# Two buffers for an expert tile's weighted output rows, and half the scratch for dynamic DMAs

## The chip, the cores and the metric

The kernel runs on one core of a Trainium2 chip. The metric is the device time of one execution in microseconds. Before the change it is 2016.36 us, the median of three runs (2011.74 to 2021.05).

## The reference

A backbone of two layers over 256 latent tokens and 256 context tokens of 1024 channels, one batch. Each layer has a token mixer (a state space, a gated MLP over chunks, differential attention, merged by gates) and then a mixture of experts. The change touches the experts alone, and of the reference they are this, for `h` of 512 tokens in the first layer and the 256 latent ones in the second:

```python
scores = jax.nn.sigmoid((h @ w_router).astype(jnp.float32))
...
_, eidx = lax.top_k(jnp.where(emask, sel, -jnp.inf), TOP_K)
wts = jnp.take_along_axis(scores, eidx, axis=1)
wts = wts / jnp.sum(wts, -1, keepdims=True) * ROUTED_SCALE
routed = routed_experts(h, eidx, wts.astype(h.dtype), w_exp_gate, w_exp_up, w_exp_down)
return routed + swiglu(h, w_sh_gate, w_sh_up, w_sh_down)
```

There are 64 experts of hidden width 256, and each token goes to 8 of them. An expert's result for a token is `(silu(x @ wg) * (x @ wu)) @ wd`, times the token's weight, and a token's results are added up. All of it is float32.

## The kernel before, in words

**Tiles.** After the router, `route` sorts the (token, expert) pairs by expert into units of 32 rows and packs four units into a tile of 128 rows. The four units use three lanes (`LANE_OF = (0, 0, 1, 2)`), so a tile takes rows of at most three experts. Large experts and small ones alternate in the order: the largest, the smallest, the second largest, and so on. With the given inputs the first layer (layer 0) has 38 tiles, the second (layer 1) 20. Per tile there is a column of token numbers to gather (`tb["gather"]`) and one of rows to add to (`tb["scatter"]`).

**Weights.** An expert's three matrices, 3 MB, are loaded by SP into one of four slots of a ring `raw` (L1226; the three DMAs of one load stand together). `load_next` (L1598) waits until the slot's former expert has been copied out (`s_cp`, L1601), and the loop at L1604 holds SP until all loads but the last have landed, so at most two are in flight.

**One tile, `body` (L1654).** On TensorE: the gate and up matmuls of tile t (`gate_up`, L1630), the transposes of tile t+1's rows (`x_t`, L1622), the transposes of the hidden values (`h_t`, L1639), then the down matmuls of tile t-1 (`down`, L1646). TensorE reads weights from `GU` (three buffers of a quarter each, per lane) and `DN` (two buffers), into which DVE (lanes 0 and 2) and ACT (lane 1) copy them from `raw` (L1578, L1584). Which slot a copy reads is loaded into registers first (`sources`, L1558; the register loads show as L1208).

The order on each engine is that of the code. On ACT, per tile: the SiLU activation of t (L1634), two copies for x_t (L1623), the copy of the hidden values (L1640), lane 1's first copy for t+1, then in `down(t-1)` the first half of y (L1648), lane 1's second copy, the second half of y, lane 1's third copy; and in the next `body` lane 1's fourth copy. On POOL, per tile: the gather of the rows of tile t+2 (L1554), then the scatter of tile t-1 (L1651), which adds the 128 rows of `Y` into `acc` in HBM; each lane adds into rows of its own. Both are dynamic DMAs, whose descriptors POOL writes; the scratch for descriptors lies at the start of every partition of SBUF.

`Y` (L1539) is one tile of 4 KB per partition:

```python
Y = pool.tile([P, D], F32, name="y")
...
nc.scalar.activation(Y[:, 512 * hf:512 * hf + 512], pY[hf], AF.Copy, scale=W[t % 4])
```

The framework puts in the waits: the first half of y waits for the landing of the scatter that read `Y` last, the scatter waits for both halves, and since every scatter adds into `acc`, for the one before.

**After the tiles,** `combine` (L1711) reads `acc` back, adds the lanes and normalizes; it begins when the last scatter has landed. In the first layer the next layer's mixer follows.

Of the kernel before, what the change touches and what calls it, by code (L numbers as in the profile page):

```python
# [11 lines left out]
F32 = mybir.dt.float32  # L12
F32R = mybir.dt.float32r
I32 = mybir.dt.int32
AF = mybir.ActivationFunctionType
ALU = mybir.AluOpType
# [5 lines left out]
P = 128  # L22
D = 1024
# [18 lines left out]
LANES = 3  # L42
# [59 lines left out]
class Build:  # L102
# [1418 lines left out]
    def experts(self, l, n, tb, fD, acc, raw):  # L1521
        nc, tc, A = self.nc, self.tc, self.A
# [8 lines left out]
        with tc.tile_pool(name="ex", bufs=1, reuse_waits="tile") as pool, \  # L1531
# [4 lines left out]
            DN = [[pool.tile([P, 2, D], F32, name="dn%d_%d" % (a, b)) for b in range(2)] for a in range(LANES)]  # L1536
            SG = pool.tile([P, EH], F32, name="sg")
            HT = [pool.tile([P, 2, P], F32, name="ht%d" % i) for i in range(2)]
            Y = pool.tile([P, D], F32, name="y")  # L1539
            W = [pool.tile([P, 1], F32, name="w%d" % i) for i in range(4)]  # L1540
            pX = [pp.tile([P, 512], F32, name="px%d" % i) for i in range(2)]
            pG = [pp.tile([P, 512], F32, name="pg%d" % i) for i in range(2)]
# [1 line left out]
            pY = [pp.tile([P, 512], F32, name="py%d" % i) for i in range(2)]  # L1544
# [97 lines left out]
            def down(t, between=()):  # L1642
                for hf in range(2):
                    for k in range(2):
                        for ln, r in rows:
                            nc.tensor.matmul(pY[hf][r, :], HT[t % 2][:, k, r], DN[ln][t % 2][:, k, 512 * hf:512 * hf + 512],  # L1646
                                             start=(k == 0), stop=(k == 1), tile_position=(0, r.start))
                    nc.scalar.activation(Y[:, 512 * hf:512 * hf + 512], pY[hf], AF.Copy, scale=W[t % 4])  # L1648
                    for f in between[hf:hf + 1]:
                        f()  # L1650
                nc.gpsimd.indirect_dma_start(out=acc, out_offset=bass.IndirectOffsetOnAxis(ap=tb["scatter"][:, t:t + 1], axis=0),  # L1651
                                             in_=Y, in_offset=None, bounds_check=LANES * n - 1, oob_is_err=False, compute_op=ALU.add)

            def body(t, sv, sa):  # L1654
                gate_up(t, range(6))
                copies_last(t, sv, sa)
                gate_up(t, range(6, KC))
                act(t)
                more = t + 1 < tmax
                if more:  # L1660
                    x_t(t + 1)
                    sv = sources(t + 1, ET.DVE, range(LANES))
                    for b in range(3):
                        for ln in (0, 2):
                            copy_gu(t + 1, ln, b, sv)
                h_t(t)
                if t + AHEAD < tmax:
                    gather(t + AHEAD)
                between = ()
                if more:  # L1670
                    sa = sources(t + 1, ET.Activation, (1,))
                    copy_gu(t + 1, 1, 0, sa)
                    between = [lambda b=b: copy_gu(t + 1, 1, b, sa) for b in (1, 2)]
                if t > 0:
                    down(t - 1, between)
                else:
                    for f in between:
                        f()
                if more:
                    for ln in (0, 1):  # L1680
                        copy_dn(t + 1, ln, sv)
                return sv, sa

            def rest(t, sv, sa):

                if t < tmax:
                    with tc.If(ntv > t) as more:
                        rest(t + 1, *body(t, sv, sa))
                    with more.Else():
                        down(t - 1)  # L1690
                else:
                    down(t - 1)
# [115 lines left out]
```

## Time and profile before

| | |
|---|---|
| median of the runs | 2016.36 us |
| the profiled execution's own time | 2016.54 us |
| its span in the trace | 2014.5 us |
| TensorE matmuls (PE) busy | 1724.2 us, 86% |
| VectorE (DVE) busy | 1153.1 us, 57% |
| ScalarE (ACT) busy | 792.6 us, 39% |
| GpSimd (POOL) busy | 585.0 us, 29% |
| HBM read and written | 403.16 MB and 55.03 MB |

Times in the trace are microseconds from the span's start. The expert tiles of the first layer run from about 640 to 1215 us, those of the second from about 1660 to 1986; the rest is the mixers, the routing and the combining. In a row of the timeline the first number is the start, the second how long it took, and the bracket at the end says how long the engine was idle before it and what ended that. PEld is TensorE's weight load. A `q` behind an engine's name is its sequencer, which waits and loads registers while the engine itself is idle. A DMA issued by POOL is busy on POOL while its descriptors are written; its landing is another, later time.

### The profile page before, as it was taken

Reading aid. Unit: us, or ns where it says so; the run is one execution under the profiler, and the core shown is the slowest. Engines: PE = TensorE matmul, PEld = TensorE weight load, DVE = VectorE, ACT = ScalarE, POOL = GpSimd, SP = SyncE. Lnnn points to the kernel's source line nnn. Section 1 sums busy time; section 2 is a strip of 40 time slices with the busy share of each in tenths; the row PEclk is TensorE's granted clock in tenths of the full one; section 3 lists DMA queues with packets and bytes.
Section 4 is the critical chain, followed back from the end, with each engine's and each line's share of the span. In section 5 each row is a group of like instructions: output and inputs, shape, how many; then the busy total and the mean of one; then the engine's idle time right before and its main releaser. Section 6 shows DMA issues by size and latency. Waiting matters only on the chain. (4 is left out here: it accounts for less than half of the span.)

```text
span 2014.5 us, 33549 instructions
## 1 busy us (share of the span) xinstructions
PE 1724.2 (86%) x12397; PEld 1009.1 (50%) x12397; DVE 1153.1 (57%) x2295; ACT 792.6 (39%) x1317; POOL 585.0 (29%) x385
## 2 busy tenths in 40 slices
PE   5898999999997988999889763889989689897883
PEld 2686866778865323333323221777779653232231
DVE  7688554333654756766565546663554456655554
ACT  3344343323313544555444343432454224443441
POOL 5355310222201324343233224323042202331222
PEclk8898999999998989999999885889999789998996
DMA  8113524553767555677798937635564567999974
GB/s 273 48 48 116 170 95 139 182 191 134 265 240 309 171 187 182 220 220 242 263 354 313 360 90 269 215 130 183 187 194 130 206 245 275 323 343 354 386 263 122
DMA packets 158391, 435.02 MB, mean 216 GB/s; under 512 B 25813, under 2 KB 82547, under 8 KB 133114
## 3 DMA queue, kind: packets, MB, share of 16 engines
q1 hardware_dynamic: 124716, 344.04, 46.5%
q0 software_dynamic: 17280, 51.93, 10.7%
q10 hardware_dynamic: 16206, 36.66, 5.0%
q8 instruction: 103, 1.69, 0.3%
q14 instruction: 86, 0.70, 0.1%
HBM read 403.16 MB, written 55.03 MB: 227 GB/s over the span
## 5 line engine op out<-in xcount | busy, mean ns | idle before, releaser
L1630 PE MATMUL pg<-gu,xt 128*32 128x512 f32 x3712 | 487.4, 641 | 105.0 <-ACT gu L1578 65.8
L1578 DVE COPY gu<-raw 128x1024 f32 x476 | 298.8, 689 | 160.0 <-issue 82.1
L1651 POOL DMA_INDIRECT acc<-y,t_scatter x58 | 208.8, 3600 | 584.0 <-ACT y L1648 313.1
L1630 PEld LDWEIGHTS pg<-gu,xt 128*32 128x32 f32 x3712 | 141.1, 117 | 438.9 <-issue 238.8
L1578 ACT COPY gu<-raw 128x1024 f32 x238 | 244.3, 1043 | 63.2 <-PE pg L1630 35.7
L1646 PE MATMUL py<-dn,ht 128*32 128x512 f32 x1856 | 211.1, 595 | 2.5 <-ACT gu L1578 1.7
L1584 DVE COPY dn<-raw 128x2048 f32 x178 | 212.9, 1224 | 0.4 <-issue 0.4
L136 PE MATMUL mm<-uh,whi 128*128 128x512 f32 (+1 forms) x544 | 199.3, 366 | 7.9 <-ACT rx L849 4.5
L138 PE MATMUL mm<-uh,wlo 128*128 128x512 f32 (+1 forms) x544 | 194.8, 358 | 0.5 <-DVE wlo L315 0.5
L137 PE MATMUL mm<-ul,whi 128*128 128x512 f32 (+1 forms) x544 | 194.2, 357 | 0.0
L315 DVE TENSOR_TENSOR wlo<-raw,whi 128x1024 fp32r<-128x1024 f32 x77 | 97.0, 1261 | 110.6 <-ACT whi L312 110.2
L312 ACT CAST whi<-raw 128x1024 fp32r<-128x1024 f32 x92 | 96.1, 1047 | 145.3 <-PE mm L137 121.3
L1648 ACT ACTIVATE y<-py,w 128x512 f32<-128x512 f32 x116 | 79.7, 689 | 157.0 <-DMA acc<-y,t_scatter 147.5
L1635 DVE TENSOR_TENSOR sg<-sg,pg 128x256 f32<-128x256 f32 x58 | 24.4, 421 | 195.7 <-ACT sg L1634 195.7
L136 PEld LDWEIGHTS mm<-uh,whi 128*128 128x128 f32 x544 | 106.3, 195 | 33.5 <-issue 8.0
L1634 ACT ACTIVATE sg<-pg 128x256 f32<-128x256 f32 x58 | 22.3, 384 | 250.1 <-PE pg L1630 250.1
L137 PEld LDWEIGHTS mm<-ul,whi 128*128 128x128 f32 x544 | 106.3, 195 | 17.1 <-issue 4.6
L1554 POOL DMA_INDIRECT xg<-f,t_gather x62 | 67.3, 1085 | 162.8 <-DVE t_scatter L1518 68.2
L138 PEld LDWEIGHTS mm<-uh,wlo 128*128 128x128 f32 x544 | 106.1, 195 | 16.1 <-issue 2.3
L1646 PEld LDWEIGHTS py<-dn,ht 128*32 128x32 f32 x1856 | 54.6, 109 | 114.9 <-issue 107.9
L1622 PEld LDWEIGHTS px<-ct,xg 128*128 128x128 f32 x480 | 58.8, 194 | 60.1 <-issue 60.1
L1622 PE MATMUL px<-ct,xg 128*128 128x128 f32 x480 | 70.4, 290 | 9.9 <-DMA xg<-f,t_gather 9.9
(482 smaller groups left out, 2823.1 us busy)
## 6 DMA issues: line engine op xcount, KB each, us to landing
raw<-in_w_exp_gate_dram SPq DMA_DIRECT2D x68, 1024.0 KB
raw<-in_w_exp_up_dram SPq DMA_DIRECT2D x68, 1024.0 KB
raw<-in_w_exp_down_dram SPq DMA_DIRECT2D x68, 1024.0 KB
raw<-in_w_in_dram SPq DMA_DIRECT2D x42, 1024.0 KB
mraw<-in_w_mod_dram SPq DMA_DIRECT2D x80, 512.0 KB
cb_y<-acc SPq DMA_DIRECT2D x18, 512.0 KB
fraw<-in_w_mod_dram SPq DMA_DIRECT2D x16, 512.0 KB
acc<-zt ACTq DMA_DIRECT2D x12, 512.0 KB
```

The costliest lines, as they stand in the source:

```text
L136: nc.tensor.matmul(out, lh, rh, start=start, stop=False)
L137: nc.tensor.matmul(out, lh, rl, start=False, stop=False)
L138: self.last = nc.tensor.matmul(out, ll, rh, start=False, stop=stop).ins
L312: self.nc.scalar.copy(hv, src)
L315: i = eng.tensor_tensor(lv, src, hv.bitcast(F32), op=ALU.subtract)
L1578: c = nc.scalar.copy(dst, gu) if ln == 1 else V.tensor_copy(dst, gu)
L1584: c = V.tensor_copy(DN[ln][t % 2].rearrange("p a b -> p (a b)"), srcs[ln][:, 4096:6144])
L1622: nc.tensor.transpose(pX[hf][:, k * P:(k + 1) * P], XG[t % AHEAD][:, 4 * hf + k:D:8], ident)
L1630: nc.tensor.matmul(pG[t % 2][r, :], XT[:, k, r], GU[ln][(4 * t + k // 2) % 3][:, k % 2].rearrange("p g n -> p (g n)"), start=(k == 0), sto ...
L1646: nc.tensor.matmul(pY[hf][r, :], HT[t % 2][:, k, r], DN[ln][t % 2][:, k, 512 * hf:512 * hf + 512], start=(k == 0), stop=(k == 1), tile_pos ...
L1648: nc.scalar.activation(Y[:, 512 * hf:512 * hf + 512], pY[hf], AF.Copy, scale=W[t % 4])
L1651: nc.gpsimd.indirect_dma_start(out=acc, out_offset=bass.IndirectOffsetOnAxis(ap=tb["scatter"][:, t:t + 1], axis=0), in_=Y, in_offset=None, ...
```

## The change

`Y` becomes two tiles that alternate from one expert tile to the next: `down` writes half by half into `Y[t % 2]`, and the scatter reads that one. The second tile takes 4 KB of every partition. The scratch for descriptors of dynamic DMAs is given as 8192 bytes per partition; without the argument it is 16384.

```diff
-            Y = pool.tile([P, D], F32, name="y")
+            Y = [pool.tile([P, D], F32, name="y%d" % i) for i in range(2)]
...
-                    nc.scalar.activation(Y[:, 512 * hf:512 * hf + 512], pY[hf], AF.Copy, scale=W[t % 4])
+                    nc.scalar.activation(Y[t % 2][:, 512 * hf:512 * hf + 512], pY[hf], AF.Copy, scale=W[t % 4])
...
                 nc.gpsimd.indirect_dma_start(out=acc, out_offset=bass.IndirectOffsetOnAxis(ap=tb["scatter"][:, t:t + 1], axis=0),
-                                             in_=Y, in_offset=None, bounds_check=LANES * n - 1, oob_is_err=False, compute_op=ALU.add)
+                                             in_=Y[t % 2], in_offset=None, bounds_check=LANES * n - 1, oob_is_err=False, compute_op=ALU.add)
...
-    nc = _bacc.Bacc("TRN2", target_bir_lowering=False, num_devices=1)
+    nc = _bacc.Bacc("TRN2", target_bir_lowering=False, num_devices=1, dynamic_dma_scratch_size=8192)
```

## Rows read from the trace of the kernel before

**Rows 1.** The page: the line that writes y, and POOL's DMA queue

```profile
L1648 ACT ACTIVATE y<-py,w 128x512 f32<-128x512 f32 x116 | 79.7, 689 | 157.0 <-DMA acc<-y,t_scatter 147.5
...
q0 software_dynamic: 17280, 51.93, 10.7%
```

**Rows 2.** Busy time by stretch; the last three columns: PE clock, DMA share, GB/s

```profile
650.00:1091.00 441.00, 399.93 (x3254) 142.61 (x3254) 277.88 (x434) 214.14 (x308) 154.00 (x61) 0.96 0.70 234
...
1667.00:1809.00 142.00, 126.95 (x1029) 46.27 (x1029) 89.46 (x140) 68.08 (x99) 44.23 (x18) 0.95 0.86 316
```

**Rows 3.** Waits of L1648 from 650.0 to 1091.2: until what, us, times

```profile
  DMA acc<-y,t_scatter: 71.2, 17
```

**Rows 4.** The timeline of ACT, 787 to 808, in part

```profile
787.67 0.38 ACT L1634 ACTIVATE sg<-pg 128x256 f32<-128x256 f32 x1 [3.74 <-PE pg L1630]
...
798.58 0.69 ACT L1648 ACTIVATE y<-py,w 128x512 f32<-128x512 f32 x1 [7.77 <-DMA acc<-y,t_scatter]
...
807.76 0.39 ACT L1634 ACTIVATE sg<-pg 128x256 f32<-128x256 f32 x1 [5.09 <-PE pg L1630]
```

**Rows 5.** The timeline of ACT, a step without the wait

```profile
749.59 0.38 ACT L1634 ACTIVATE sg<-pg 128x256 f32<-128x256 f32 x1 [4.67 <-PE pg L1630]
...
761.49 0.38 ACT L1634 ACTIVATE sg<-pg 128x256 f32<-128x256 f32 x1 [4.04 <-PE pg L1630]
```

**Rows 6.** The timeline of ACT: layer 0's tiles 0, 31; layer 1's tiles 0, 8

```profile
650.01 0.38 ACT L1634 ACTIVATE sg<-pg 128x256 f32<-128x256 f32 x1 [2.73 <-PE pg L1630]
...
1091.27 0.39 ACT L1634 ACTIVATE sg<-pg 128x256 f32<-128x256 f32 x1 [2.98 <-PE pg L1630]
...
1666.89 0.39 ACT L1634 ACTIVATE sg<-pg 128x256 f32<-128x256 f32 x1 [4.23 <-PE pg L1630]
...
1778.85 0.38 ACT L1634 ACTIVATE sg<-pg 128x256 f32<-128x256 f32 x1 [3.92 <-PE pg L1630]
```

**Rows 7.** The timeline of POOL: two scatters and a gather

```profile
755.64 6.03 POOL L1651 DMA_INDIRECT acc<-y,t_scatter  x1 [9.39 <-DVE gu L1578]
761.98 1.04 POOL L1554 DMA_INDIRECT xg<-f,t_gather  x1 [0.30 <-issue]
...
1039.51 4.92 POOL L1651 DMA_INDIRECT acc<-y,t_scatter  x1 [10.50 <-DVE dn L1584]
```

**Rows 8.** The timeline of DVE: the last copies beside those two scatters

```profile
758.99 1.22 DVE L1584 COPY dn<-raw 128x2048 f32 x1
...
1041.75 1.22 DVE L1584 COPY dn<-raw 128x2048 f32 x1
```

**Rows 9.** ACT's register loads, from 761.5 and from 787.7: ns min/median/max, starts

```profile
L1208 ACTq TENSOR_LOAD <-t_unit x1: 1664/1664/1664, 762.9 to 762.9; - x1
...
L1208 ACTq TENSOR_LOAD <-t_unit x1: 493/493/493, 789.1 to 789.1; - x1
```

**Rows 10.** The chain that ended last, at layer 1's last scatters

```profile
1968.90 7.80 DMA acc<-y,t_scatter
...
1976.72 0.02 POOLq L1651
...
1978.35 8.00 DMA acc<-y,t_scatter
```

**Rows 11.** SP's issues: first and last of 25 loads, and of 17

```profile
686.36 0.34 SPq L1226 DMA_DIRECT2D raw<-in_w_exp_gate_dram  x1
...
1089.52 0.34 SPq L1226 DMA_DIRECT2D raw<-in_w_exp_gate_dram  x1
...
1778.09 0.34 SPq L1226 DMA_DIRECT2D raw<-in_w_exp_gate_dram  x1
...
1933.21 0.34 SPq L1226 DMA_DIRECT2D raw<-in_w_exp_gate_dram  x1
```

**Rows 12.** Issue to landing: all scatters; gathers of layer 0

```profile
DMA to landing us min/median/max: 5.9/10.7/16.3
...
DMA to landing us min/median/max: 4.4/10.1/12.8
```

## The prediction

> **What bounds the kernel now.** I read the costliest groups on the profile's page first. The ACT line that writes y has 79.7 us of work and stands idle 157.0 us before it, 147.5 of them until a scatter of earlier rows has landed [rows 1]. Idle time counts only on the path, so the timeline of ACT came next. With the wait: the SiLU activation of one tile starts at 787.67, y is stalled 7.77 us until 798.58, and the next tile's activation comes at 807.76, 20.09 us after the first [rows 4]. Without it the same step goes from 749.59 to 761.49, 11.90 us [rows 5]. The cause is the order on ACT: lane 1's copies of the next tile (L1578) are queued behind y, and the gate/up matmuls need those copies. So the wait stops TensorE.
>
> How much of it is in the total? Layer 0's tiles 0 to 31 have their activations at 650.01 and 1091.27: 441.26 us for 31 steps [rows 6]. At 11.90 each they would take 368.9. The excess is 72.4 us, and the same stretch shows 71.2 us of ACT waiting on scatters [rows 3]. Here the wait is nearly the whole excess. The DMA engines are busy for a share of 0.70 there, against 0.86 early in layer 1 [rows 2]: room for the expert weights to come sooner in layer 0, little in layer 1. At the end of both layers each tile needs two or three new experts, and loads set the pace: in layer 1, from 1778.09 to 1933.21, 17 loads are issued, 155.1 / 16 = 9.7 us apart [rows 11].
>
> **The change, part by part.** The profiled execution took 2016.54 us, 0.18 over the median of the three runs (2016.36), so the sum holds for both.
>
> *The second y.* y of a tile now waits for the scatter of two tiles before. With steps of 11.9 us that one has been out for over 20 us, and the longest landing is 16.3 [rows 12]. ACT's wait goes; I price what is left of it at nothing.
>
> What is late next is the scatter itself. Scatters still add into one array, and POOL has its own wait for the earlier one: in the chain that ended last, a scatter lands at 1968.90 + 7.80 = 1976.70 and POOL's sequencer at L1651 passes 0.02 us later, before ACT has written anything [rows 10]. That wait, so far covered by ACT's, becomes POOL's. Behind it on POOL stands the gather of a later tile. So one scatter at a time has to fit into 11.9 us. Writing its descriptors takes 6.03 us if it starts at 755.64 and 4.92 if it starts at 1039.51 [rows 7]; DVE's last copy ends at 758.99 + 1.22 = 760.21 and at 1041.75 + 1.22 = 1042.97 [rows 8]. Both writings end 1.46 us after that copy (761.67, 1044.43). A late start therefore costs nothing as long as it comes before DVE's pause. The data then need at most 16.3 - 6.0 = 10.3 us [rows 7, 12], and 10.3 + 1.46 = 11.8 is just under 11.9: it fits, with no room. The gather goes out 0.49 us after the activation (761.98 against 761.49) [rows 5, 7], lands in a median of 10.1 us and at most 12.8 [rows 12], and is needed about 11.8 after the activation. Cost 0, at worst 1.5 us for some tiles.
>
> One cost is new. A scatter that starts beside the copies moves its data just as DVE and ACT load the next tile's registers. In the step from 761.49, with no expert load in flight, ACT's register load takes 1.66 us; in the step from 787.67, beside an expert load, 0.49 [rows 9]. The copies wait for it, so such a step lasts 11.90 + 1.17 = 13.07. I saw this only where no expert load ran beside it. In layer 0's stretch 25 loads are issued, the first at 686.36 and the last at 1089.52 [rows 11]; at 9.7 us they cover 242 of the new 382 us, 0.63. That leaves 11 of 31 steps at 13.07: 13 us given back (from 0 to 31 x 1.17 = 36.3). Layer 0: 72.4 - 13 = 59.4.
>
> Layer 1: the eight steps from 1666.89 to 1778.85 take 111.96 us, 16.8 over 8 x 11.90 = 95.2 [rows 6]. There the DMA engines idle for a share of only 0.14 [rows 2], 15.7 us of 112, and loads can't be squeezed by more. I take 13, between 5 and 16.8. After that, as in layer 0 after tile 31, loads go at their 9.7 us, and a later tile gains only that everything is shifted forward: 0, at best 10 in gaps.
>
> At a layer's end two scatters follow each other with nothing to hide them. Now a landing at 1976.70 is followed by two y activations and the next writing at 1978.35 [rows 10], 1.65 us. With y ready only POOL's wait remains; I take 1.3 saved per layer, 2.6 in all (0 to 3.3).
>
> *The scratch.* No instruction is added. What a fuller ring costs no row shows. The queue moved 17280 packets [rows 1] for 58 scatters and 62 gathers, 144 each, 9 on each of 16 DMA engines; at most a scatter and two gathers are in flight, since each scatter waits for the one before. Below, a stall of every gather until the scatter ahead has landed would make it some 10 us late; above, nothing. I take 0, as the queue is this short; I exclude a gain, since nothing waits for room now. The Trainium skill (DMA: Bandwidth & Descriptors, "The descriptor swizzle" and "Terms") gives 9 read and 9 write descriptors of 16 bytes per engine for such a transfer, so that by it 8192 bytes hold some 56 transfers; the packets agree with the 9, the capacity no run here shows.
>
> *Addresses.* Tiles on the left of SBUF move down by 8 KB, so waits of one tile for the former owner of its place may come or go in the mixers: 0, within 4 us either way.
>
> **Sum:** 59.4 + 13 + 2.6 = 75 us. 2016.5 - 75 = 1941.5.
>
> **The rivals.**
> *Smaller gain, 1976 us.* Every scatter now stands where the register loads are slow, and expert loads in flight don't help: 31 steps of 13.07 = 405.2, layer 0 gains 36; layer 1 gains 5, the ends 0. 2016.5 - 41 = 1976. For it: the slow step follows a scatter beside DVE's copies, which becomes the rule. Against: beside an expert load the register load took 0.49 us [rows 9].
> *Slower, 2049 us.* The place is POOL at L1651: if a late writing of descriptors takes its 6.03 us over again, instead of ending with DVE's pause, one scatter under expert loads needs 16.3 + 0.2 = 16.5 us per tile, and the chain of scatters is the bound. It decides from where this exceeds today's mean step of 441.26 / 31 = 14.2. Layer 0: 31 x (0.63 x 16.5 + 0.37 x 11.9) = 459, 18 more than now; layer 1: 8 x (0.86 x 16.5 + 0.14 x 11.9) = 127, 15 more. 2016.5 + 33 = 2049. Against: the two writings that end 1.46 us after DVE's copies [rows 7, 8].
> *No change, 2016 us.* The wait only changes its owner: scatters land no more often than now, one per 14.2 us, the two buffers fill, and ACT waits again for the older one. For it: POOL's own wait [rows 10] and landings of up to 16.3 us [rows 12]. Against: the median landing is 10.7 [rows 12], and a writing of 6.03 us contains 4.57 us of DVE's copies (755.64 to 760.21) [rows 7, 8], which a later start leaves out. The Trainium skill (DMA: Bandwidth & Descriptors, "Rules for kernel authors") demands just that order: an accumulating DMA has to wait for the earlier one's semaphore; the trace agrees, and by it alone a second buffer would buy nothing once scatters are the bound.
> *Larger gain, 1918 us.* No slow register loads, and layer 1's loads follow fully: 72.4 + 16.8 + 3.3 + some 6 in late gaps = 98.
>
> **How the numbers follow.** The forecast (1925 to 1962) gets 0.58, the smaller gain (1962 to 1990) 0.22, the larger 0.08, no change 0.06, slower 0.06. The range of 8 in 10 is 1912 to 1984: it takes the forecast and nearly all of the smaller gain, with 4 us for the addresses, and reaches to the larger one; no change and slower are left out. Measurement of this kernel tells about 0.5% (10 us) from no change: faster by more 0.88, within 0.06, slower 0.06.
>
> **What would show it.** Right: ACT's idle time before y until a scatter falls from 147.5 us to under 20; POOL's wait before L1651 ends at landings; most steps of layer 0 up to tile 31 last 11.9 or 13.1, and their sum is near 382; the late loads stay near 9.7 us apart. The register loads' median says whether the smaller gain holds. Wrong: scatters that start after DVE's pause and write for 6 us again; TensorE waiting for gathers at L1622; loads in layer 0 that hold the copies back before tile 31; or gathers that start only when scatters have landed, which would be the scratch.

## The result, and the profile after

The changed kernel takes 1944.01 us, the median of four runs (1935.97 to 1952.69), against 2015.56 for the kernel before (2011.74 to 2021.05): a ratio of 0.9644, 95% interval 0.9594 to 0.9694. Run again later it gave 1943.07. The forecast was 1941.5, with 1912 to 1984 as its range. The profiled execution took 1940.67 us, with a span of 1938.6 against 2014.5. The number is right; several of the terms behind it are not, and the wait that the change removed had a second cause that the forecast did not see.

From the page of the kernel after: the line that writes y, the scatter, the transposes that wait for a gather, and POOL's queue.

```profile
q0 software_dynamic: 17280, 51.93, 10.9%
...
L1651 POOL DMA_INDIRECT acc<-y,t_scatter x58 | 181.1, 3122 | 548.8 <-DVE gu L1578 289.9
...
L1622 PE MATMUL px<-ct,xg 128*128 128x128 f32 x480 | 72.0, 295 | 35.6 <-DMA xg<-f,t_gather 35.0
L1648 ACT ACTIVATE y<-py,w 128x512 f32<-128x512 f32 x116 | 79.8, 688 | 23.4 <-PE py L1646 15.0
```

ACT's idle time before y fell from 157.0 us, 147.5 of them behind scatters [rows 1], to 23.4, and a scatter is no longer what it waits for. A new wait has come on TensorE: the transposes of L1622 wait for gathers. In all it is 75.7 us (35.0 in front of matmuls, the rest in front of weight loads), where the kernel before had 9.9.

Where the 75.9 us of span came from is read off the starts of L1634 on ACT. After: layer 0's tiles 0 and 31, layer 1's tiles 0 and 19.

```profile
650.78 0.38 ACT L1634 ACTIVATE sg<-pg 128x256 f32<-128x256 f32 x1 [2.73 <-PE pg L1630]
...
1047.04 0.38 ACT L1634 ACTIVATE sg<-pg 128x256 f32<-128x256 f32 x1 [4.04 <-PE pg L1630]
...
1605.49 0.38 ACT L1634 ACTIVATE sg<-pg 128x256 f32<-128x256 f32 x1 [2.98 <-PE pg L1630]
...
1890.30 0.38 ACT L1634 ACTIVATE sg<-pg 128x256 f32<-128x256 f32 x1 [4.04 <-PE pg L1630]
```

| stretch (us) | before | after | gain | forecast |
|---|---|---|---|---|
| layer 0, tiles 0 to 31 | 441.3 | 396.3 | 45.0 | 59.4 |
| layer 0, tiles 31 to 37 (expert loads) | 98.6 | 99.4 | -0.8 | 0 |
| from there to layer 1's first tile | 477.1 | 459.1 | 18.0 | 1.3 |
| layer 1, all 19 steps | 294.6 | 284.8 | 9.8 | 13 |
| from the last tile to the end | 53.0 | 48.3 | 4.7 | 1.3 |

Busy time by stretch after, columns as in [rows 2]; the first is layer 0's tiles 0 to 31, the second the first 142 us of layer 1's experts:

```profile
650.78:1047.04 396.26, 376.69 (x3255) 141.51 (x3256) 280.79 (x434) 216.64 (x308) 133.05 (x60) 0.99 0.77 260
1605.50:1747.50 142.00, 128.80 (x1117) 49.55 (x1118) 96.77 (x152) 76.41 (x108) 39.60 (x20) 0.98 0.92 343
```

The DMA engines' share rose from 0.70 to 0.77 and from 0.86 to 0.92: the same expert weights in less time. Layer 1's early steps had some room, less than was forecast.

The waits of L1622 in layer 0's tiles 0 to 31 after, and ACT's register loads there (ns min/median/max):

```profile
  DMA xg<-f,t_gather: 41.1, 23
```

```profile
L1208 ACTq TENSOR_LOAD <-t_unit x31: 475/503/1677, 652.2 to 1036.6; - x31
```

The register loads keep their median of 0.5 us, and four of 31 take over 1 us (six before). The rival of a smaller gain, in which all of them would be slow, is out.

Three things were left to explain: layer 0 gained 14 us less than forecast, the stretch between the layers 17 us more, and the gathers come late.

### The profile page after: what moved, and what is told of

Its sections match the earlier page's. It is cut to its first block, busy times and chain, and to the rows that moved or that the text cites. A ratio compares the mean times of both kernels' runs of the same rounds, so it can differ in the third digit from the quotient of the medians.

```text
span 1938.6 us, 33538 instructions
## 1 busy us (share of the span) xinstructions
PE 1684.7 (87%) x12397; PEld 1002.2 (52%) x12397; DVE 1156.3 (60%) x2295; ACT 797.5 (41%) x1317; POOL 558.7 (29%) x385
## 3 DMA queue, kind: packets, MB, share of 16 engines
q1 hardware_dynamic: 124716, 344.04, 48.3%
## 5 line engine op out<-in xcount | busy, mean ns | idle before, releaser
L1630 PE MATMUL pg<-gu,xt 128*32 128x512 f32 x3712 | 451.0, 619 | 55.8 <-DVE gu L1578 51.4
L1578 DVE COPY gu<-raw 128x1024 f32 x476 | 300.3, 693 | 181.4 <-SPq L1238 89.6
L1651 POOL DMA_INDIRECT acc<-y,t_scatter x58 | 181.1, 3122 | 548.8 <-DVE gu L1578 289.9
L1578 ACT COPY gu<-raw 128x1024 f32 x238 | 246.9, 1042 | 93.6 <-PE pg L1630 66.8
L136 PE MATMUL mm<-uh,whi 128*128 128x512 f32 (+1 forms) x544 | 197.6, 363 | 8.5 <-ACT rx L849 4.6
L138 PE MATMUL mm<-uh,wlo 128*128 128x512 f32 (+1 forms) x544 | 193.8, 356 | 0.7 <-DVE wlo L315 0.5
L1634 ACT ACTIVATE sg<-pg 128x256 f32<-128x256 f32 x58 | 22.2, 383 | 256.4 <-PE pg L1630 252.4
L136 PEld LDWEIGHTS mm<-uh,whi 128*128 128x128 f32 x544 | 105.7, 194 | 34.1 <-issue 7.2
L138 PEld LDWEIGHTS mm<-uh,wlo 128*128 128x128 f32 x544 | 105.5, 194 | 15.9 <-issue 1.8
L1622 PEld LDWEIGHTS px<-ct,xg 128*128 128x128 f32 x480 | 60.1, 195 | 86.9 <-issue 46.2
L1622 PE MATMUL px<-ct,xg 128*128 128x128 f32 x480 | 72.0, 295 | 35.6 <-DMA xg<-f,t_gather 35.0
L1648 ACT ACTIVATE y<-py,w 128x512 f32<-128x512 f32 x116 | 79.8, 688 | 23.4 <-PE py L1646 15.0
```

The lines of the kernel that those rows point to most:

```text
L136: nc.tensor.matmul(out, lh, rh, start=start, stop=False)
L138: self.last = nc.tensor.matmul(out, ll, rh, start=False, stop=stop).ins
L1578: c = nc.scalar.copy(dst, gu) if ln == 1 else V.tensor_copy(dst, gu)
L1622: nc.tensor.transpose(pX[hf][:, k * P:(k + 1) * P], XG[t % AHEAD][:, 4 * hf + k:D:8], ident)
L1630: nc.tensor.matmul(pG[t % 2][r, :], XT[:, k, r], GU[ln][(4 * t + k // 2) % 3][:, k % 2].rearrange("p g n -> p (g n)"), start=(k == 0), sto ...
L1648: nc.scalar.activation(Y[t % 2][:, 512 * hf:512 * hf + 512], pY[hf], AF.Copy, scale=W[t % 4])
```

## The experiments

Each is timed against the kernel before, in the same rounds on the same chip (there it took 2014.9 to 2019.3 us, so runs of different rounds are compared by their ratios; 1% is 20 us). "Scatters over 5 us" are those of 58 whose descriptors take POOL that long to write. The last four columns come from one profile each: layer 0's tiles 0 to 31, the stretch between the layers' experts, layer 1's steps, and that count.

| run | y buffers | scratch | us | ratio (95%) | layer 0 | between | layer 1 | scatters over 5 us |
|---|---|---|---|---|---|---|---|---|
| before | 1 | 16384 | 2015.6 | | 441.3 | 477.1 | 294.6 | 22 |
| after | 2 | 8192 | 1944.0 | 0.964 (0.959-0.969) | 396.3 | 459.1 | 284.8 | 15 |
| after_again | 2 | 8192 | 1943.1 | 0.965 (0.963-0.967) | 394.0 | 457.2 | 284.9 | 13 |
| s8_only | 1 | 8192 | 2003.1 | 0.991 (0.988-0.994) | 438.9 | 470.6 | 294.0 | 22 |
| y2_s12 | 2 | 12288 | 1957.1 | 0.971 (0.968-0.974) | 391.5 | 469.9 | 285.1 | 15 |
| gather_early | 2 | 8192 | 1925.3 | 0.954 (0.951-0.957) | 379.2 | 459.4 | 284.2 | 2 |
| both_early | 2 | 8192 | 1928.3 | 0.955 (0.952-0.958) | 378.7 | 465.3 | 283.1 | 0 |
| y1_gather_s8 | 1 | 8192 | 1955.5 | 0.970 (0.968-0.973) | 405.6 | 463.3 | 288.3 | 0 |
| y1_gather | 1 | 16384 | 1970.0 | 0.976 (0.974-0.979) | 402.5 | 479.0 | 290.9 | 0 |
| pool_touch | 2 | 8192 | 1924.0 | 0.955 (0.952-0.958) | 375.9 | 456.2 | 287.1 | 0 |
| touch_late | 2 | 8192 | 1941.4 | 0.964 (0.961-0.967) | 393.8 | 463.0 | 284.5 | 14 |
| dve_shift | 2 | 8192 | 1921.2 | 0.951 (0.948-0.955) | 379.6 | 456.7 | 285.0 | 0 |
| y1_shift | 1 | 16384 | 1954.9 | 0.967 (0.964-0.970) | 390.2 | 474.1 | 287.4 | 0 |
| shift_far | 2 | 8192 | 1922.5 | 0.951 (0.947-0.954) | 380.2 | 459.6 | 284.1 | 0 |

The same kernel gives layer 0 within 2.3 us in two profiles and its median within 1 us (after, after_again); differences of less than some 5 us in one profile's stretch are not read.

What was expected of the second run of after: 

> The changed kernel again, beside the runs above and the same runs of the kernel before, to see how far one profile's stages and the median move by themselves: the median between 1936 and 1953, layer 0's tiles 0 to 31 at 396 +- 5 us, layer 1's 19 steps at 285 +- 2, the stretch between them at 459 +- 6.

### The two halves of the change

s8_only has the smaller scratch alone:

```diff
-    nc = _bacc.Bacc("TRN2", target_bir_lowering=False, num_devices=1)
+    nc = _bacc.Bacc("TRN2", target_bir_lowering=False, num_devices=1, dynamic_dma_scratch_size=8192)
```

> One buffer for the rows as before, the scratch for dynamic DMAs at 8,192 as after. In this program the second layer's mixer is ordered exactly as after the change, the expert stages as before it. Theory: the stretch between the layers' experts got some 18 us shorter in two parts, 14 by the other order in the second layer's mixer, which comes with the smaller scratch alone, and 4 to 5 by the earlier end of the last scatters, which comes with the second buffer. Then both expert stages stay at 441 and 295 us, the stretch between the layers goes from 477 to about 463, and the time is 2015.6 - 14 = about 2001. Rival 1 (the order costs the same, the 14 us came with the second buffer): the stretch stays at 477 and the time at 2015. Rival 2 (half of the scratch leaves too little room for descriptors, hidden after by the second buffer): L1651 on POOL waits or writes longer, the expert stages grow and the time is over 2015.

y2_s12 has the second buffer, as in after, with `dynamic_dma_scratch_size=12288`.

> Two buffers for the rows, the scratch at 12,288 instead of 8,192; in this program the expert stages are ordered as after the change and the second layer's mixer as before it. Theory: the experts' gain and the ends of the layers are those of after (layer 0's tiles 0 to 31 in 396 us, layer 1's first 19 steps in 285), the stretch between the layers is 477 - 4.5 = about 472 instead of 459, and the time is 1944 + 14 = about 1958. Rival 1 (the mixer's 14 us came with the second buffer): 1944. Rival 2 (a smaller scratch holds the scatters back): layer 0 gets shorter than 396 us and the time is below 1944.

Measured: ratios of 0.9911 and 0.9706. They multiply to 0.962, and the whole is 0.9644. So 12 to 18 us of the change's 72 (0.9706 less 0.9644; 1 less 0.9911) are not the second buffer's: they come with the scratch of 8192, and in the profile between the layers. (Two runs further down differ by the scratch alone as well, y1_gather and y1_gather_s8: 0.9762 less 0.9701, again 12 us.) The order of instructions in layer 1's mixer is another one there. The timeline of PE before, at the place where the two part:

```profile
1335.74 0.77 PE L803 MATMUL tr<-ct,yb 128*128 128x128 f32 x2 [4.86 <-DVE yb L800]
...
1338.28 1.06 PE L687 MATMUL y<-s5h,CK 128*128 128x64 f32 x4
```

The same in s8_only:

```profile
1337.55 0.30 PE L803 MATMUL tr<-ct,yb 128*128 128x128 f32 x1 [1.47 <-DVE yb L800]
...
1338.15 0.27 PE L803 MATMUL tr<-ct,yb 128*128 128x128 f32 x1
1338.26 0.60 PE L851 MATMUL att<-rx,ctr 128*128 128x256 f32 x2
...
1340.93 0.61 PE L687 MATMUL y<-s5h,CK 128*128 128x64 f32 x4
```

Before, the transposes L803 stand ahead of the projection's matmuls (L136 to L138) and TensorE sits 4.86 us for their input. In s8_only, as in after, projection matmuls stand ahead of them and leave 1.47 us of that wait. The rest is put down to the clock. Busy time by stretch, before and then s8_only; PEclk is the third column from the right:

```profile
1330.80:1335.70 4.90, 0.08 (x4) 0.00 (x0) 4.90 (x12) 0.00 (x0) 1.30 (x1) 0.79 0.34 107
1335.70:1343.00 7.30, 6.57 (x29) 6.08 (x29) 2.10 (x7) 3.02 (x6) 1.35 (x2) 0.50 0.81 271
1343.00:1350.00 7.00, 7.00 (x24) 6.03 (x24) 0.42 (x1) 0.98 (x3) 0.73 (x1) 0.50 0.50 161
```

```profile
1332.00:1338.00 6.00, 4.53 (x43) 3.17 (x32) 6.00 (x14) 1.28 (x1) 1.91 (x1) 1.00 0.56 169
1338.00:1345.00 7.00, 7.00 (x52) 6.50 (x51) 3.83 (x7) 2.85 (x7) 2.78 (x4) 1.00 0.58 193
```

Behind the idle stretch TensorE runs at 0.50, its level of 1.2 GHz, for the 14 us shown; in s8_only, without the long idle stretch, it stays at 2.4 GHz, and the same four matmuls of L687 take 0.61 us instead of 1.06. The first L851, a matmul of the attention, comes 161.4 us after layer 0's last activation before, 154.6 in y2_s12, 147.2 in s8_only and 142.5 in after. 12 to 14 us of that go with the scratch and 5 to 7 with the second buffer. An estimate from these rows: 14 us at half the clock hold the work of 7, and with the 3.4 us less of waiting (4.86 less 1.47) that is some 10 of the 12 to 14. In all ten profiles with 8192 this distance is 140.5 to 147.2 us, in the four others 154.6 to 161.4. In s8_only part of it is given back later, since its whole stretch is only 6.4 us shorter (that profile is of the slowest of its six runs, 2009.2 us). Rival 1, that all of this came with the second buffer, is out. Rival 2 of both runs, a scratch that holds scatters back, shows nowhere: 22 and 15 writings over 5 us as in before and after, and landings with medians of 10.7 us in all three of before, s8_only and y2_s12.

### The gather, one tile earlier

```diff
                 if more:
                     x_t(t + 1)
+                    if t + 1 + AHEAD < tmax:
+                        gather(t + 1 + AHEAD)
...
-                if t + AHEAD < tmax:
-                    gather(t + AHEAD)
...
             x_t(0)
+            gather(AHEAD)
```

> After, with the gather of a tile's tokens issued one tile earlier: right behind the transposes that free its buffer and ahead of the scatter of the tile before. Theory: the transposes of L1622 waited 76 us in all for gathers that lay behind a scatter's data, some 13 of them in layer 0; issued some 10 us earlier they land in time, those waits fall under 20 us, layer 0's tiles 0 to 31 take about 383 us instead of 396, layer 1 a few us less, and the time is 1944 - 15 = about 1929 (give or take what another order in the mixers makes, read by stage). Rival 1 (the queue is full with scatters, expert loads and gathers, and the early gather only pushes a scatter back by as much): layer 0 stays at 396 us, the waits move to L1651 and L1648 and the time at 1944. Rival 2 (the scatter now waits on POOL behind a gather that waits for the transposes, and is written later): y's wait for scatters comes back and the time is over 1950.

both_early adds to this:

```diff
-                act(t)
                 more = t + 1 < tmax
                 if more:
+                    sv = sources(t + 1, ET.DVE, range(LANES))
+                    sa = sources(t + 1, ET.Activation, (1,))
+                act(t)
+                if more:
                     x_t(t + 1)
...
-                    sv = sources(t + 1, ET.DVE, range(LANES))
...
-                    sa = sources(t + 1, ET.Activation, (1,))
```

> After, with the gather one tile earlier and with the register loads of VectorE and ScalarE for the next tile moved ahead of the tile's activation L1634, away from the stretch in which a scatter's data moves. Theory: the steps of 13.2 to 14.1 us in layer 0 without an expert load in flight, some 5 of them, are long by register loads of 1.7 to 2.1 us instead of 0.5; moved, they lose that, 5 to 6 us in all; with the gathers' 15 the time is about 1923 and layer 0's tiles 0 to 31 take about 377 us. Rival 1 (a register load is slow at any place when a scatter is in flight, and one always is): no more gain than by the early gather alone. Rival 2 (the loads now stand ahead of the activation and delay it by 0.5 us in every step): 0.5 x 58 = 29 us more than by the early gather alone.

Measured: 1925.3 and 1928.3 (both issue one gather more per layer, 64 instead of 62). The page of gather_early:

```profile
L1651 POOL DMA_INDIRECT acc<-y,t_scatter x58 | 142.2, 2451 | 254.9 <-DVE gu L1578 89.4
...
L1622 PE MATMUL px<-ct,xg 128*128 128x128 f32 x480 | 70.4, 290 | 10.5 <-DMA xg<-f,t_gather 10.5
```

The wait for gathers is back at 10.5 us, and layer 0 is 17 us shorter, more than the 13 expected: 27 of its 31 steps last 11.90 to 11.92. The slow register loads went too but for one of 1.07 us, though nothing was done about them. They had not been slow by their place in the step as such: in after every one over 1 us begins 0.5 to 1.6 us behind the end of a scatter's writing. Most loads there are fast all the same, and what parts them is what the prediction named, the expert loads. Over all 14 profiles, layer 0's tiles 0 to 31: of the register loads of ACT and VectorE that begin 0.3 to 2.1 us behind such an end, 73 of 74 took over 1 us where no packet of the expert loads' queue (q1) had begun in the microsecond before, and 16 of 337 where one had; of the other 1325, none. In both_early, where VectorE's loads were moved so that they come 0.6 to 1.8 us behind that end, 18 of 93 take 1.3 to 2.1 us. So moving them gained nothing, and rival 2's 29 us, from loads that delay every activation, did not come either.

What I had not expected stands in the first row: the mean writing of a scatter fell from 3.12 us to 2.45. The writings of 6 us are gone but for two.

y1_gather_s8 and y1_gather take the second buffer away from that kernel, the latter with the whole scratch (it is the kernel before with the early gather and nothing else).

> The early gather with one buffer for the rows again, scratch 8,192: but for that buffer and the waits on it, the same program as the early gather alone. Open: whether the second buffer is needed at all once the gather is out of the way. Theory A: with the early gather a scatter is written in 2.9 us instead of 6.05 and lands 1.7 to 2.7 us after the next tile's activation, ahead of y at 3.3 us, so that y finds its single buffer free: layer 0's tiles 0 to 31 stay at about 380 us, and the time is that of the early gather, 1925 to 1932. Theory B: a scatter that begins later than 6.05 us after the activation, behind a copy or an expert load, lands too late, y waits for it and delays the next one, as in the kernel before: every second step is 18 to 20 us, layer 0's tiles 0 to 31 are back at 430 to 440 us, and the time is 1925 + 60 = about 1985.

> The kernel before with the early gather alone: one buffer, the whole scratch, the second layer's mixer ordered as before. Theory A of the run above: the experts as with the early gather (380 and 284 us), the stretch between the layers some 13 us longer by the mixer's order: 1925 + 13 = about 1938, faster than the change itself without any of its two parts. Theory B: about 2000, as the kernel before with the gather's few late landings gone.

Measured 1955.5 and 1970.0, between both theories. In y1_gather_s8 ACT still waits for scatters, in the answer on L1648:

```profile
  DMA acc<-y,t_scatter: 100.9, 24
```

So with the early gather the second buffer is worth 0.9701 - 0.9537 = 0.0164, some 33 us, where it was worth 0.9911 - 0.9644 = 0.0267, some 54 us, in the change. And the early gather, on the kernel before, takes 2.4% or 48 us off without a second buffer. The 147.5 us of waiting that the prediction gave to the one buffer had another cause besides.

### What makes a scatter's writing 6 us long

In the kernels before and after, a scatter in an undisturbed step (one of some 11.9 us) begins 6.05 us after the activation and is written for 6.02 to 6.07 us; with the early gather at the same place of the step, beside the same copies, for 2.93. First a copy of 128x1 numbers on POOL, to see if POOL's having worked shortly before is what counts:

```diff
                     x_t(t + 1)
+                    nc.gpsimd.tensor_copy(WT, W[(t + 1) % 4])
```

> After, with one copy of 128x1 numbers added on POOL in every step, which waits for W of the next tile and so runs some 1.1 us after the activation, where the early gather stood; every other engine's instructions are those of after. Asked: why the scatter at 6.05 us after the activation, beside the same copies of VectorE, was written in 2.93 us with the early gather and in 6.04 us in after. Theory A: what counts is that POOL had worked shortly before: the scatters are written in about 2.9 us, land some 3 us earlier, the gathers behind them too, and the time falls by some us below 1944. Theory B: what counts is the gather itself, or the order of gather and scatter: the scatters with no gather before them still take 6.04 us, and the time is 1944 or a little more.

It gave 1924.0, but by its wait it also held the gather back into the step, behind the copy and ahead of the scatter. The timeline of POOL in it (L1555 and L1652 are the gather and the scatter, a line lower by the line added):

```profile
677.94 0.18 POOL L1663 COPY wt<-w 128x1 f32<-128x1 f32 x1 [4.10 <-DVE xg L1626]
678.77 1.12 POOL L1555 DMA_INDIRECT xg<-f,t_gather  x1 [0.64 <-PE ph L1640]
682.82 2.92 POOL L1652 DMA_INDIRECT acc<-y,t_scatter  x1 [2.93 <-ACT y L1649]
```

So the run told nothing between a busy POOL and a gather ahead. touch_late leaves the gather in its place behind the scatter:

```diff
                 if t + AHEAD < tmax:
                     gather(t + AHEAD)
+                nc.gpsimd.tensor_copy(WT, HT[t % 2][:, 0, 0:1])
```

> After, with one copy of 128x1 numbers on POOL in every step behind the gather and ahead of the scatter, which waits for the tile's HT and so runs 2 to 3.5 us after the activation; gathers keep their place right behind the scatter before, which the copy of the run pool_touch did not leave them (there the gather itself came to lie at 1.97 us after the activation, between that copy and the scatter). Asked again: what makes the scatter at 6.05 us be written in 2.9 instead of 6.04 us. Theory A (POOL had worked shortly before): 2.9 us here too, the scatters land some 3 us earlier, the gathers behind them are issued 3 us earlier, and layer 0's tiles 0 to 31 come near 376 to 385 us, the time near 1930. Theory B (a gather between two scatters in the same step): the scatters at 6.05 still take 6.04 us, layer 0 stays at 394 to 396 us and the time at 1943.

```profile
689.38 0.18 POOL L1670 COPY wt<-ht 128x1 f32<-128x1 f32 x1 [4.60 <-ACT ht L1641]
693.32 6.04 POOL L1652 DMA_INDIRECT acc<-y,t_scatter  x1 [3.75 <-DVE gu L1579]
699.67 1.05 POOL L1555 DMA_INDIRECT xg<-f,t_gather  x1 [0.31 <-issue]
```

POOL works 3.75 us ahead of the scatter, and it is written for 6.04 us all the same; the time is 1941.4. A busy POOL is not it. Over all runs the ends of the writings that meet copies show a pattern: most end either 0.08 us behind the end of one of VectorE's copies, which is 0.16 us behind the start of the next, or 1.46 to 1.49 us behind the end of the last copy of the step. The 6 us writings are of the second kind. In an undisturbed step a copy of L1578 begins some 2.75 us after the scatter. In before, after and the other runs with long writings the median of that distance is 2.746 to 2.749 us; in gather_early, y1_gather, y1_gather_s8 and pool_touch it is 2.765 to 2.767. To move VectorE's copies and nothing else, a memset of 128x1 numbers was put among them:

```diff
                 if more:
+                    V.memset(WT, 0.0)
                     for ln in (0, 1):
                         copy_dn(t + 1, ln, sv)
```

> After, with one memset of 128x1 numbers on VectorE in every step, ahead of the two copies of the down weights, so that the copies behind it begin some 0.06 to 0.1 us later; nothing else differs, gathers and scatters keep their places on POOL. In all runs so far a scatter's writing that meets VectorE's copies ends either 0.16 us behind the start of one of them or 1.46 to 1.49 us behind the end of the last. In after a scatter begins 6.05 us after the activation, the copies of gate and up at 2.75 and 3.35 us after that: the first is missed and the writing ends at 6.04; with the early gather and in the run pool_touch the same copies lay at 2.76 to 2.82 us and the writing ended at 2.93. Theory (what decides is whether the writing is ready when a copy of VectorE ends, and 2.75 us is some 10 ns too early): with the copies at 2.82 or later the scatters are written in about 3.0 us instead of 6.04, they land 3 us earlier, the next gather stands behind them and is issued 3 us earlier, layer 0's tiles 0 to 31 come to 376 to 385 us and the time to about 1930. Rival (the gather's place on POOL decides, and the times of VectorE's copies only went along): 6.04 us as before, 394 to 396 us, 1943.

> The kernel before (one buffer, whole scratch) with the same memset on VectorE and nothing else. Theory: there too a scatter of the undisturbed step begins at 6.05 and is written until 12.1, lands at 16.6 or later, 4.7 us into the next step, and that is what y at 3.3 us waits for; written in about 3.0 us it lands ahead of y as in the run y1_gather, so that most of the 147 us of L1648's wait on scatters goes: layer 0's tiles 0 to 31 in 400 to 410 us instead of 441 and a time near 1970 to 1975. Rival: 441 us and 2015, the wait for the scatter is the same however the copies lie.

dve_shift took 1921.2 us, the fastest of all and 0.9514 of the kernel before; y1_shift, the kernel before with that memset alone, 1954.9, a ratio of 0.967 where the whole change has 0.964. The timelines of POOL and of VectorE, first after, then dve_shift (whose lines lie one lower):

```profile
694.96 6.04 POOL L1651 DMA_INDIRECT acc<-y,t_scatter  x1 [8.54 <-DVE gu L1578]
701.30 1.04 POOL L1554 DMA_INDIRECT xg<-f,t_gather  x1 [0.30 <-issue]
```

```profile
697.11 1.29 DVE L1578 COPY gu<-raw 128x1024 f32 x2
698.31 1.22 DVE L1584 COPY dn<-raw 128x2048 f32 x1
```

```profile
691.89 2.95 POOL L1652 DMA_INDIRECT acc<-y,t_scatter  x1 [7.19 <-DVE wt L1681]
695.14 1.47 POOL L1555 DMA_INDIRECT xg<-f,t_gather  x1 [0.31 <-issue]
```

```profile
694.06 1.30 DVE L1579 COPY gu<-raw 128x1024 f32 x2
695.28 1.21 DVE L1585 COPY dn<-raw 128x2048 f32 x1
```

In after the first of the two copies of L1578 begins 697.11 - 694.96 = 2.15 us behind the scatter's start and the second 0.6 us later; the writing goes on to 701.00, which is 1.47 behind the last copy's end (698.31 + 1.22 = 699.53). In dve_shift they come at 2.17 and some 2.78, and the writing ends at 694.84, in the middle of the copies. The gather that stands behind it on POOL is issued 3 us sooner in the step. The long writings are gone in both runs, layer 0 takes 379.6 us with two buffers and 390.2 with one, and no register load of ACT or VectorE there is over 1 us.

shift_far puts the memset 2.5 us ahead of the scatter, between two pairs of gate/up copies, so that the memset itself is over when the scatter begins:

```diff
                     for b in range(3):
+                        if b == 1:
+                            V.memset(WT, 0.0)
                         for ln in (0, 2):
```

> As the run dve_shift, but the memset of 128x1 stands some 2.5 us ahead of the scatter, between the first and the second pair of VectorE's copies of gate and up, instead of 0.1 us ahead of it. Theory (the place of the copies' ends against the writing decides): the copies behind it begin some 0.03 us later as in dve_shift, the writing ends at 2.9 us again, layer 0's tiles 0 to 31 in about 380 us, the time about 1921. Rival (the memset itself, just ahead of the scatter, lets POOL in): here it is long over when the scatter begins, the writing takes 6.04 us again, layer 0 is back at 394 to 396 us and the time at 1943. A third outcome stays possible: if the copies wait for something else behind the memset and do not move, the time is 1943 too, and the starts of the copies show it (2.75 us after the scatter's start).

1922.5 us, the copies' median distance 2.774, and the scatters written in 2.94:

```profile
697.18 2.94 POOL L1652 DMA_INDIRECT acc<-y,t_scatter  x1 [7.20 <-DVE gu L1579]
700.43 1.47 POOL L1555 DMA_INDIRECT xg<-f,t_gather  x1 [0.30 <-issue]
```

So a memset on VectorE, in either of two places, ends the long writings, and so does an early gather; touch_late, with the same extra tile and a busy POOL, does not.

That they do it by shifting the copies is likely but not shown, and the shift ahead of the writing's end is smaller than the distances above. Take the scatters that begin 6.03 to 6.07 us after the activation, with the two copies of L1578 2.1 to 2.9 us behind them. The second copy starts 0.601 to 0.604 us behind the first beside all 84 long writings, and 0.610 to 0.622 beside all 132 short ones of 2.92 to 3.01 us. That is so elsewhere too: in every run, a copy of L1578 that starts 0.10 to 0.23 us ahead of the end of a writing of POOL starts at least 0.608 us after the copy before it, where the median of pairs with no such writing near is 0.602 or 0.603. So 8 ns or more of the 16 to 35 that the second copy's medians lie apart go with the short writing itself, and need not be what brings it about. The first copy, which starts some 0.8 us before a short writing ends, has medians of 2.144 to 2.147 us in the runs with long writings and 2.152 to 2.161 in the others, 5 to 17 ns apart, and no value parts them: the best, 2.149, leaves 29 of 216 on the wrong side. What on POOL has to be ready when a copy ends is not seen in a trace, and so the reason for the two lengths stays open.

The Trainium skill (SBUF — State Buffer, "SBUF: two separate sides" and, under it, "A bandwidth-pool intuition that's wrong (but worth ruling out)") says that VectorE's fp32 copies between SBUF tiles lock GpSimd out of a port pair that the two share, so that a DMA issued from POOL waits with its descriptors until such a copy ends plus some 115 ns. The short writings agree, with 0.08 us. The long ones do not: they let the ends of four copies pass and end 1.46 us or more behind the last, and here the measurement decides.

## Why the prediction was right or wrong

**The wait and the second y: right in kind.** ACT's wait for scatters fell from 147.5 us to nothing. But the text took the 6.03 us of writing as given, with "Writing its descriptors takes 6.03 us if it starts at 755.64". It hangs on something as small as a memset of 0.06 us on VectorE: y1_shift shows that 3.3% could be had so, with one buffer and the whole scratch. The second buffer is worth 54 us where the writings are long (s8_only against after). Where they are short it is worth 33 with the early gather (y1_gather_s8 against gather_early), and less with the memset: y1_shift and dve_shift lie 0.9671 - 0.9514 = 0.0157, 32 us, apart, and 12 to 18 of these are the scratch's, which leaves 14 to 20.

**Layer 0, forecast 59.4, measured 45.0.** The step that failed is the gathers' "Cost 0, at worst 1.5 us for some tiles". Behind a long writing they did go out some 0.5 us after the activation, as forecast, but they landed as late as 14.4 us after their issue, where the longest before was 12.8 [rows 12]; 23 waits at L1622 add up to 41.1 us in the stretch, and the steps that they lengthen last up to 15.9 us. The excess over 31 x 11.90 is 396.3 - 368.9 = 27.4 us instead of the 13 forecast for register loads. By steps: 11.7 in six that wait for gathers alone, 6.1 in three with a late gather and slow register loads, 2.9 in two with slow register loads alone, 5.1 in one of 17.0 us whose copies wait 5.8 us for an expert load, and 1.5 in the rest. dve_shift, without long writings, has next to nothing left of the first three, so both the late gathers and the slow register loads go with the long writings. Its own excess of 10.7 is nearly all one step of 22.4, an expert load that is not there yet: the forecast let loads "cover 242 of the new 382 us" and hold nothing up before tile 31, but the last ones there already set the pace. With TensorE's waits at L1622 these are two of the forecast's own signs of being wrong.

**Register loads, 13 us: the mechanism right, the size not.** They are slow in the first two microseconds behind a scatter's writing, with its data on the way and no expert load beside it, as forecast. That came about in 5 of 31 steps, not 11, and those five exceed 11.90 by 9.1 us in all, 6.1 of them in the three that wait for a gather too.

**A late writing ends with VectorE's pause: right, by half.** Of the 42 scatters in after that start more than 6.1 us after the activation, 39 are written in 1.57 to 3.10 us, as in this row of the timeline of POOL after, and three in 4.45 to 5.56. So the slower rival's 6.03 us over again did not come, and POOL's own wait for the scatter before is 62.7 us in eight times.

```profile
711.66 1.59 POOL L1651 DMA_INDIRECT acc<-y,t_scatter  x1 [9.32 <-DVE dn L1584]
```

The other half, that a writing beside copies has to wait for their pause, is false: it can end between two of them.

**Layer 1, forecast 13, measured 9.8:** the 13 were put in the first eight steps, and these gained 5.7 (106.2 us instead of 112.0); the later ones, put at 0, gained 4.1. Loads set the pace of most steps from the eighth on, and no run brought the stretch below 283.

**The ends of the layers, forecast 2.6, measured 4.7 at the last and 4.8 at the first** (TensorE's first matmul of the combination, L1725, begins 16.0 us after the last activation instead of 20.8). The chain that ended last after, against [rows 10]:

```profile
1884.46 10.74 DMA acc<-y,t_scatter
...
1897.02 7.52 DMA acc<-y,t_scatter
...
1905.34 5.83 DMA acc<-y,t_scatter
...
1912.18 5.82 DMA cb_y<-acc
```

From the last landing but one, 1897.02 + 7.52 = 1904.54, to the next scatter it is 0.80 us instead of 1.65, and one scatter earlier 1.82 (1895.20 to 1897.02) instead of 2.57 (1966.33 to 1968.90 in that chain before): 1.6 together where 1.3 was forecast. The term was too small mainly because the last transfer itself took 5.83 us instead of 8.00.

**Addresses, "0, within 4 us either way": wrong.** The instructions' order in layer 1's mixer changed with the size of the scratch, for 18.0 - 4.8 = 13 us of this profile and 12 to 18 by s8_only and y2_s12. That it would be those places that matter could not be read from the trace of before; that TensorE's clock fell behind the wait of 4.86 us there could.

**The scratch's ring, 0: right.** Scatters landed after a median of 10.7 us with half of it, as with the whole (s8_only, before).

So the forecast's 75 us were 59.4 + 13 + 2.6, and the measured 75.9 are 45.0 + 9.8 + 9.5, some 13 of an order that no step had priced, and 1.6 lost before and behind layer 0's first 31 steps. Layer 0's 14 us too much and the mixer's 13 too little cancelled.

**The rivals.** No change and slower fell with the scatters' late writings; the smaller gain with the register loads' median. The larger gain's 1918 us assumed no slow register loads; dve_shift and shift_far, where there are none and three, come near it with 1921 and 1922.

## What to carry to other kernels

When a wait ends at a transfer, look at why that transfer takes so long before buying a buffer for it: here the long part was the writing of its descriptors, and one instruction of 0.06 us per step on another engine removed it. Ask of a duration that occurs at only two values, 2.9 and 6.0 us at the same place of the step, what makes the difference, and price both. And where a change moves addresses or sizes, compare the order of instructions outside of the change too, and put work that is ready ahead of a matmul that will wait: here the wait cost its own length and the clock behind it.

## What was not expected of the hardware

Most descriptor writings on POOL beside back-to-back copies on VectorE ended 0.08 us behind the end of a copy or 1.46 to 1.49 us behind the last one, and one memset of 0.06 us per step among the copies turned the 6.04 us of the undisturbed steps into some 2.94. Register loads of 0.5 us, on ACT and VectorE alike, took over 1 us and up to 2.1 when they began 0.3 to 2.1 us behind the end of a scatter's writing with no expert load moving data: 73 of 74, against 16 of 337 with one. TensorE, after 4.9 us with almost nothing to do (0.08 us busy), ran at 1.2 GHz for the next 14 us although it was busy for most of them.
